# Weighting the first half's attention groups at the out-projection's operands, and its recurrent gates behind a later load

## The chip, the cores and the metric

One Trainium2 chip, one of its cores. The metric is the device time of one execution in microseconds (us). Engines are named as in the profile: PE (TensorE), DVE (VectorE), ACT (ScalarE), POOL (GpSimd), SP (SyncE, which here only issues DMAs). Each engine works through its own queue in order.

## What is computed

One layer over 2048 tokens of width 1024. The part that matters here is how the attention groups meet the output projection, and the gates of the recurrent mixer:

```python
def attention_mixer(q, k, v):                 # three groups g of two heads
    ...
    o = jnp.stack(outs, axis=2)
    lse = jnp.stack(lses, axis=2)
    alpha = jax.nn.softmax(lse, axis=2)       # shares of the groups
    return (o * alpha[..., None]).reshape(B, S, ATTN_WIDTH).astype(q.dtype)

def rg_lru(x, w_a, b_a, w_x, b_x, lam):
    r = jax.nn.sigmoid(jnp.einsum("bshi,hio->bsho", xh, w_a).reshape(B, S, C) + b_a)
    i = jax.nn.sigmoid(jnp.einsum("bshi,hio->bsho", xh, w_x).reshape(B, S, C) + b_x)
    ...                                       # a scan over the tokens
    mix = jnp.concatenate([y_attn, y_conv, y_lru], axis=-1)
    x = x + jnp.einsum("bsc,cd->bsd", mix, w_out)
    h2 = rmsnorm(x, norm2_g)
    ff = jnp.square(jax.nn.relu(jnp.einsum("bsd,df->bsf", h2, w_up)))
    return x + jnp.einsum("bsf,fd->bsd", ff, w_down)
```

## The kernel before

Activations lie with channels on the 128 partitions and tokens along the free axis. The tokens go in two halves h of 1024 (HS), each half in two blocks m of 512 (NB). Every float32 product is three matmuls of rounded halves: an operand is cast on ACT to its high half and DVE subtracts to get the low half (`split`, L242 and L243, in the input projection; `halves`, L907 and L908, behind it).

The order of the program: the input projection of half 0; then that of half 1, with the mixers of half 0 beside it; then output projection, up and down projections, with the mixers of half 1 as side work. The input projection's results are evacuated from PSUM by DVE (L388 to L395). In this stretch a planner lays out every engine's queue from priorities; the mixers of half 0 carry an offset that fills them in between the main matmuls. Within the mixers of half 0 the order is attention, convolution, recurrent mixer (`lru_mixer`), `combine`.

`combine` turns the statistics of the softmax, which it loads from `sscr` (L802), into the shares of the three groups and stores these to DRAM in `wscr` (L827). It then loads them back, broadcast over 64 partitions (L841), with each group's output from `oscr` (L843), multiplies on DVE (L834) and stores the product to `mscr` (L850, L854). `act_load` (L922) fetches `mscr` for the output projection into `rounded` slots, where `act_split` halves it.

`lru_mixer` takes three channel tiles t. It loads x from `lscr` (L542) and the gate weights from `gates_w` (L543), does a four-tap convolution on DVE (L548, L552), splits u block by block, runs two gates of three matmuls for each block on PE (L564 to L566), loads the GeLU branch from `gscr` (L571), and then does the scan (L582). `conv_ahead` loads the convolution input of half 1 from `uscr` (L464) and runs 31 taps on DVE (L472, L474) ahead of half 1's mixers. The values of half 1 are projected at L425 to L427, the last part of the input projection.

Small tiles come from a pool of 15 (`mtile`, `mtile_r`), large ones from a pool of 8 (`wide`). SP issues nearly all DMAs of half 0, POOL the key loads of the attention (L603, L612, L622) and the mixer loads of half 1; two copies of weights, `out_w` and `down_w`, are issued by ACT (L1590, L1591). A DMA signals one of eight semaphores of its kind (DMAHW0 to DMAHW7 for SP and ACT, DMASW0 to DMASW7 for POOL), taken in turn in the order in which the program issues them. An issue whose semaphore is still owed by an earlier DMA waits for that one.

Of the kernel before, what the change touches and what calls it, by code (L numbers as in the profile page):

```python
# [79 lines left out]
def body(tc, xt, w_in, w_v, w_out, w_up, w_down, vecs, lru_wa, lru_wx, consts, g_row, out, out_rows):  # L80
# [51 lines left out]
    def work(h):  # L132
        return wide_tile() if h == 0 else mtile()
# [4 lines left out]
    def work_pair(h):  # L138
        if h == 0:
            t = wp.tile([P, HS + 32], F32R, name="wr", tag="W")  # L140
            return t[:, :NB], t[:, NB:HS]
        return tuple(mp.tile([P, 544], F32R, name="mr", tag="M")[:, :NB] for _ in range(2))
# [310 lines left out]
    def loads(h):  # L453
        return nc.gpsimd if h else nc.sync
# [78 lines left out]
    def mtile_r():  # L533
        return mp.tile([P, 544], F32R, name="mr", tag="M")[:, :NB]

    def lru_mixer(h):
        n = HS if h == 0 else NB
        for t0 in range(h * HS, (h + 1) * HS, n):
            for t in range(3):
                x = work(h)  # L540
                gw = mtile_r()
                loads(h).dma_start(x[:, :n + 3], lscr[t][:, t0 + 29:t0 + n + 32])  # L542
                loads(h).dma_start(gw[:, :NB].bitcast(F32), gates_w[t])  # L543
                u = work(h)[:, :n]
                if h:
                    yield 0
                    yield 0
                nc.vector.tensor_scalar(u, x[:, 0:n], v("lru_conv_w", t * LTAPS), v("lru_conv_b", t), op0=OP.mult, op1=OP.add)  # L548
                for k in range(1, LTAPS):
                    if k == 2:  # L550
                        yield 1.3
                    nc.vector.scalar_tensor_tensor(u, x[:, k:k + n], v("lru_conv_w", t * LTAPS + k), u, op0=OP.mult, op1=OP.add)  # L552
                yield 1.5
                r, i = work(h)[:, :n], work(h)[:, :n]
                for c in range(0, n, NB):
                    uh, ul = work_pair(h)
                    split(u[:, c:c + NB], uh, ul)
                    yield 0.7
                    yield 0
                    for m, (dst, name) in enumerate(((r, "lru_ba"), (i, "lru_bx"))):  # L560
                        bank = mix_bank() if h and m else conv_bank()
                        wh, wl = (gw[:, part * P:(part + 1) * P] for part in (m, 2 + m))
                        with first():
                            nc.tensor.matmul(bank, wh, uh, start=True, stop=False)  # L564
                            nc.tensor.matmul(bank, wh, ul, start=False, stop=False)
                            nc.tensor.matmul(bank, wl, uh, start=False, stop=True)  # L566
                        nc.scalar.activation(dst[:, c:c + NB], bank, AF.Sigmoid, bias=v(name, t))
                    yield 0
                nc.vector.tensor_mul(u, u, i)
                gg = work(h)[:, :n]  # L570
                loads(h).dma_start(gg, gscr[t][:, t0:t0 + n])  # L571
                a = work(h)[:, :n]
                nc.scalar.activation(a, r, AF.Exp, scale=splus[:, 12 + t:13 + t])
                nc.scalar.activation(r, r, AF.Tanh, scale=splus[:, 9 + t:10 + t])
                yield 0.7
                nc.scalar.activation(i, a, AF.Square)
                nc.vector.scalar_tensor_tensor(r, i, 1.0, r, op0=OP.add, op1=OP.mult)
                nc.scalar.activation(r, r, AF.Sqrt)
                yield 0.7
                nc.vector.tensor_mul(u, u, r)  # L580
                init = 0.0 if t0 == 0 else state[:, t:t + 1]
                nc.vector.tensor_tensor_scan(i, a, u, init, OP.mult, OP.add)  # L582
                if t0 + n < S:
                    nc.vector.tensor_copy(state[:, t:t + 1], i[:, n - 1:n])
                yield 2.1
                nc.vector.tensor_mul(gg, gg, i)
                yield 0.7
                stores(h).dma_start(mscr[5 + t][:, t0:t0 + n], gg)
# [204 lines left out]
    def combine(h):  # L793
# [31 lines left out]
        for g in range(3):  # L825
            for j in range(2):
                stores(h).dma_start(wscr[g][j, t0:t0 + HS].rearrange("(c w) -> c w", w=16), m[j * HD:(j + 1) * HD, g, :])  # L827
        yield 0
        parts = [(b, g) for b in range(2) for g in range(3)]
        held = []  # L830

# [68 lines left out]
    def lo(i):  # L900
        return X(i)[:, NB:]

    def f32(a):
        return a.bitcast(F32)
# [10 lines left out]
    def out_at(n):  # L915
        return 1 - n // 4 % 2, n % 4 + n // 8 * 4

    def act_load(h, m, n0, n1):
        i, t0 = ACTS[m] + n0, h * HS + m * NB
        k = MIX_ORDER[n0]  # L920
        dst = rounded[i // 4].rearrange("p (s b n) -> p s b n", s=4, b=2)[:, i % 4:i % 4 + n1 - n0, 1, :]
        nc.sync.dma_start(f32(dst), mscr[k:k + n1 - n0, :, t0:t0 + NB].rearrange("k p n -> p k n"))  # L922

    def act_split(m, n):
        i = ACTS[m] + n
        halves(f32(lo(i)), hi(i), lo(i))

    def out_pair(w, pairs):
        if w in (2, 3):
# [790 lines left out]
```

## Time and profile before

| | |
|---|---|
| median of 3 runs | 2002.42 us (2000.58 to 2003.43) |
| the profiled execution, its time | 1999.48 us |
| its span, first to last instruction | 1997.7 us |
| granted TensorE clock, mean | 0.996 |
| instructions | 25490 |

The profiled execution is 2.9 us below the median, and 1.8 us of it lie around its span. Times in a timeline are from the start of the span. The stretch that the change touches lies between 255 and 510 us, the input projection of half 1, and between 490 and 530 us, the start of the output projection.

### The profile page before, as it was taken

The page shows a single profiled execution, that of the slowest core. Times are in us where ns is not written, and L with a number is a line of the kernel's source. Part 1 is how long each engine was busy: PE and PEld are TensorE (multiplying, and loading weights), DVE is VectorE, ACT ScalarE, POOL GpSimd, SP SyncE. Part 2 cuts the span into 40 slices and gives each one's busy share as a digit, 9 for nine tenths or more (in the row PEclk, how much of TensorE's full clock was granted, in tenths as well). Part 3 has the DMA queues.
Part 4 walks back from the last instruction along what each step waited for, and adds up shares of the span by engine and source line. Part 5 has one row for each costly group of instructions (what it writes and reads, how often), then busy time and mean ns, then how long its engine had stood idle before and what let it go on. Part 6 is the DMA issues. An engine that isn't in the chain of part 4 may idle for free.

```text
span 1997.7 us, 25490 instructions
## 1 busy us (share of the span) xinstructions
PE 1956.4 (98%) x8906; PEld 1593.7 (80%) x8906; DVE 1450.5 (73%) x1976; ACT 1050.4 (53%) x1634; POOL 168.2 (8%) x297
## 2 busy tenths in 40 slices
PE   8999998999999999999999999999999999999998
PEld 6887776789777777888888878788888888888886
DVE  7899785794567665887969899867555555577884
ACT  6144875513556764556656566446545555444343
POOL 0023200000022423000000000100000000000001
PEclk9999999999999999999999999999999999999999
DMA  5555596635555646544788777764444447786773
GB/s 169 165 151 159 165 294 196 216 121 165 182 168 164 196 151 217 193 154 162 271 286 279 249 275 248 245 199 146 158 153 151 145 143 262 240 293 215 263 260 136
DMA packets 202124, 399.78 MB, mean 200 GB/s; under 512 B 25382, under 2 KB 33814, under 8 KB 201932
## 3 DMA queue, kind: packets, MB, share of 16 engines
q1 hardware_dynamic: 182548, 342.02, 51.0%
q0 software_dynamic: 16096, 45.38, 7.8%
q10 hardware_dynamic: 3352, 10.76, 1.6%
q8 instruction: 70, 1.15, 0.2%
q14 instruction: 58, 0.48, 0.1%
HBM read 287.47 MB, written 119.00 MB: 203 GB/s over the span
## 4 chain that ended last, share of the span: by engine, by line
PE 82%; DVE 7%; DMA 5%; ACT 3%; issue 2%; SPq 0%; POOL 0%; DVEq 0%; ACTq 0%
PE bank L1135 10%; PE bank L1136 10%; PE bank L1137 10%; PE bank L1497 8%; PE bank L1498 8%; PE bank L1499 8%; PE mm L265 4%; PE mm L262 4%; PE mm L268 4%; PE bank L948 2%; PE bank L949 2%; PE bank L950 2%; DVE wide L474 1%; PE mm L425 1%; PE mm L427 1%
## 5 line engine op out<-in xcount | busy, mean ns | idle before, releaser
L1135 PE MATMUL bank<-rounded,pair 128*128 128x512 f32 x896 | 353.1, 394 | 2.8 <-ACT low L1144 2.2
L1136 PE MATMUL bank<-rounded,pair 128*128 128x512 f32 x896 | 351.7, 393 | 0.0
L1137 PE MATMUL bank<-rounded,pair 128*128 128x512 f32 x896 | 351.3, 392 | 0.0
L1497 PE MATMUL bank<-rounded,rounded 128*128 128x512 f32 x688 | 268.3, 390 | 1.7 <-DVE z L1510 1.4
L1499 PE MATMUL bank<-rounded,rounded 128*128 128x512 f32 x688 | 268.1, 390 | 0.0
L1498 PE MATMUL bank<-rounded,rounded 128*128 128x512 f32 x688 | 268.1, 390 | 0.0
L908 DVE TENSOR_TENSOR rounded<-rounded 128x1024 fp32r<-128x1024 f32 (+1 forms) x172 | 186.5, 1097 | 74.7 <-ACT rounded L907 73.6
L907 ACT CAST rounded<-rounded 128x1024 fp32r<-128x1024 f32 (+1 forms) x172 | 160.9, 949 | 134.5 <-DMA rounded<-fscr 102.8
L1135 PEld LDWEIGHTS bank<-rounded,pair 128*128 128x128 f32 x896 | 168.8, 188 | 41.5 <-ACT low L1144 2.6
L1137 PEld LDWEIGHTS bank<-rounded,pair 128*128 128x128 f32 x896 | 168.4, 188 | 35.9
L1136 PEld LDWEIGHTS bank<-rounded,pair 128*128 128x128 f32 x896 | 168.6, 188 | 34.9 <-issue 0.2
L262 PE MATMUL mm<-rounded,rounded 128*128 128x512 f32 x496 | 159.5, 397 | 8.4 <-ACT rounded L242 7.1
L268 PE MATMUL mm<-rounded,rounded 128*128 128x512 f32 x496 | 159.1, 396 | 0.0
L265 PE MATMUL mm<-rounded,rounded 128*128 128x512 f32 x496 | 157.4, 394 | 0.0
L907 ACT CAST rounded<-kept 128x1024 fp32r<-128x1024 f32 x80 | 84.1, 1051 | 133.7 <-DVE kept L1307 66.1
L1497 PEld LDWEIGHTS bank<-rounded,rounded 128*128 128x128 f32 x688 | 129.2, 188 | 29.3 <-DVE z L1510 1.8
L1499 PEld LDWEIGHTS bank<-rounded,rounded 128*128 128x128 f32 x688 | 129.2, 188 | 27.4 <-DVE rounded L908 0.4
L1498 PEld LDWEIGHTS bank<-rounded,rounded 128*128 128x128 f32 x688 | 129.2, 188 | 26.7
L242 ACT CAST rounded<-raw 128x512 fp32r<-128x512 f32 (+1 forms) x96 | 55.6, 582 | 146.8 <-PE mm L265 92.7
L907 ACT CAST pair<-wraw 128x1024 fp32r<-128x1024 f32 x64 | 67.1, 1048 | 117.1 <-PE bank L1136 111.2
L908 DVE TENSOR_TENSOR rounded<-kept,rounded 128x1024 fp32r<-128x1024 f32 x80 | 97.8, 1222 | 39.6 <-ACT rounded L907 39.3
L908 DVE TENSOR_TENSOR pair<-wraw,pair 128x1024 fp32r<-128x1024 f32 x64 | 78.2, 1222 | 60.6 <-ACT pair L907 60.5
(371 smaller groups left out, 3727.4 us busy)
## 6 DMA issues: line engine op xcount, KB each, us to landing
fscr<-low SPq DMA_DIRECT2D x224, 256.0 KB, 2.1
rounded<-fscr SPq DMA_DIRECT2D x112, 512.0 KB, 4.2
second<-in_w_down SPq DMA_DIRECT2D x80, 512.0 KB, 5.7
kept<-in_w_down SPq DMA_DIRECT2D x48, 512.0 KB, 5.4
raw<-in_w_in SPq DMA_DIRECT2D x64, 256.0 KB, 4.0
low<-in_w_up SPq DMA_DIRECT2D x64, 256.0 KB, 3.1
wraw<-in_w_up SPq DMA_DIRECT2D x64, 256.0 KB, 3.0
raw<-in_xt SPq DMA_DIRECT2D x32, 256.0 KB, 3.5
```

The source lines that it names most:

```text
L242: nc.scalar.copy(h, raw)
L262: nc.tensor.matmul(bank, wh[:, sl], ah[:, cols], start=first_, stop=False)
L265: nc.tensor.matmul(bank, wh[:, sl], al[:, cols], start=False, stop=False)
L268: nc.tensor.matmul(bank, wl[:, sl], ah[:, cols], start=False, stop=last_)
L907: nc.scalar.copy(h, raw)
L908: nc.vector.tensor_sub(l, raw, f32(h))
L1135: nc.tensor.matmul(bank, wh[:, sl], hi(x), start=fresh and k == 0, stop=False, **kw)
L1136: nc.tensor.matmul(bank, wh[:, sl], lo(x), start=False, stop=False, **kw)
L1137: nc.tensor.matmul(bank, wl[:, sl], hi(x), start=False, stop=k == KH - 1, **kw)
L1497: nc.tensor.matmul(banks[j], th[:, c], sh[:, x], start=fresh and k0, stop=False, **kw)
L1498: nc.tensor.matmul(banks[j], th[:, c], sl[:, x], start=False, stop=False, **kw)
L1499: nc.tensor.matmul(banks[j], tl[:, c], sh[:, x], start=False, stop=k1, **kw)
```

## The change

Two things change for half 0, and one of them also for half 1.

`combine(0)` ends with the stores of the shares to `wscr`. `act_load` puts the raw outputs of the groups from `oscr` straight into the operand slots (on SP) and loads the broadcast shares on POOL's queue into small tiles; `act_split` multiplies by the share (DVE) and halves the product. So the six L843 loads, the six `mscr` stores and two 768 KB loads go, six 256 KB loads on SP come; the twelve 128 KB broadcasts move from SP to POOL; the six multiplications stay, three of them now in the output projection's start.

`lru_mixer` splits both blocks of u first, then loads `gscr`, and then runs the gates; for half 0 the first matmul of each gate is planned behind that load by an order edge without a semaphore.

```diff
--- before.py
+++ after.py
@@ -533,6 +533,10 @@
     def mtile_r():
         return mp.tile([P, 544], F32R, name="mr", tag="M")[:, :NB]
 
+    def behind(i, other):
+        tc.add_manual_dep(i.ins, other.ins.name, mybir.DependencyInfo(
+            mybir.DependencyClass.NoSync, mybir.DependencyReason.DATA), reason="order")
+
     def lru_mixer(h):
         n = HS if h == 0 else NB
         for t0 in range(h * HS, (h + 1) * HS, n):
@@ -552,23 +556,28 @@
                     nc.vector.scalar_tensor_tensor(u, x[:, k:k + n], v("lru_conv_w", t * LTAPS + k), u, op0=OP.mult, op1=OP.add)
                 yield 1.5
                 r, i = work(h)[:, :n], work(h)[:, :n]
+                split_u = []
                 for c in range(0, n, NB):
-                    uh, ul = work_pair(h)
-                    split(u[:, c:c + NB], uh, ul)
+                    split_u.append(work_pair(h))
+                    split(u[:, c:c + NB], *split_u[-1])
                     yield 0.7
                     yield 0
+                gg = work(h)[:, :n]
+                loaded = loads(h).dma_start(gg, gscr[t][:, t0:t0 + n])
+                for c in range(0, n, NB):
+                    uh, ul = split_u[c // NB]
                     for m, (dst, name) in enumerate(((r, "lru_ba"), (i, "lru_bx"))):
                         bank = mix_bank() if h and m else conv_bank()
                         wh, wl = (gw[:, part * P:(part + 1) * P] for part in (m, 2 + m))
                         with first():
-                            nc.tensor.matmul(bank, wh, uh, start=True, stop=False)
+                            mm = nc.tensor.matmul(bank, wh, uh, start=True, stop=False)
+                            if h == 0:
+                                behind(mm, loaded)
                             nc.tensor.matmul(bank, wh, ul, start=False, stop=False)
                             nc.tensor.matmul(bank, wl, uh, start=False, stop=True)
                         nc.scalar.activation(dst[:, c:c + NB], bank, AF.Sigmoid, bias=v(name, t))
                     yield 0
                 nc.vector.tensor_mul(u, u, i)
-                gg = work(h)[:, :n]
-                loads(h).dma_start(gg, gscr[t][:, t0:t0 + n])
                 a = work(h)[:, :n]
                 nc.scalar.activation(a, r, AF.Exp, scale=splus[:, 12 + t:13 + t])
                 nc.scalar.activation(r, r, AF.Tanh, scale=splus[:, 9 + t:10 + t])
@@ -826,6 +835,8 @@
             for j in range(2):
                 stores(h).dma_start(wscr[g][j, t0:t0 + HS].rearrange("(c w) -> c w", w=16), m[j * HD:(j + 1) * HD, g, :])
         yield 0
+        if h == 0:
+            return
         parts = [(b, g) for b in range(2) for g in range(3)]
         held = []
 
@@ -915,15 +926,30 @@
     def out_at(n):
         return 1 - n // 4 % 2, n % 4 + n // 8 * 4
 
+    shares = {}
+
     def act_load(h, m, n0, n1):
         i, t0 = ACTS[m] + n0, h * HS + m * NB
         k = MIX_ORDER[n0]
+        if h == 0 and k < 3:
+            for n in range(n0, n1):
+                g = MIX_ORDER[n]
+                nc.sync.dma_start(f32(lo(ACTS[m] + n)), oscr[g][:, t0:t0 + NB])
+                w = shares[m, n] = mtile()[:, :NB]
+                for j in range(2):
+                    nc.gpsimd.dma_start(w[j * HD:(j + 1) * HD, :], wscr[g][j:j + 1, t0:t0 + NB].to_broadcast([HD, NB]))
+            return
         dst = rounded[i // 4].rearrange("p (s b n) -> p s b n", s=4, b=2)[:, i % 4:i % 4 + n1 - n0, 1, :]
         nc.sync.dma_start(f32(dst), mscr[k:k + n1 - n0, :, t0:t0 + NB].rearrange("k p n -> p k n"))
 
     def act_split(m, n):
         i = ACTS[m] + n
-        halves(f32(lo(i)), hi(i), lo(i))
+        x = f32(lo(i))
+        if (m, n) in shares:
+            w = shares.pop((m, n))
+            nc.vector.tensor_mul(w, w, x)
+            x = w
+        halves(x, hi(i), lo(i))
 
     def out_pair(w, pairs):
         if w in (2, 3):
```

On SP's queue, around the first load of gate weights, this stands before (names as in the text above; `raw` are input-projection weights):

```order
L922 DMA rounded_79<-mscr 128x2x512 [waits DMAHW5_49,DMAHW7_49,DMAHW3_49,PE_49]
L399 DMA uscr<-z 128x1024 [waits DMAHW4_49,DVE_49]
L251 DMA raw_102<-in_w_in 128x512 [waits DVE_49]
L251 DMA raw_103<-in_w_in 128x512 [waits DMAHW6_49,DVE_49]
L790 DMA sscr<-stat_142 512x1x4 [waits DVE_49,Activation_49]
L790 DMA sscr<-stat_142 512x1x4 [waits DMAHW0_49]
L543 DMA mr<-gates_w 128x512 [waits DMASW4_49,DMASW3_49,DMASW7_49,DMASW2_49,DMAHW1_49,DMASW1_49,DMASW0_49]
```

and this after the change (L943 is the old L922, L566 the old L571, L799 the old L790, L547 the old L543):

```order
L943 DMA rounded_79<-mscr 128x2x512 [waits DMAHW5_49,DMAHW7_49,DMAHW1_49,PE_49]
L566 DMA wide<-gscr 128x1024 [waits DMAHW6_49]
L399 DMA uscr<-z 128x1024 [waits DVE_49]
L251 DMA raw_102<-in_w_in 128x512 [waits DMAHW0_49,DVE_49]
L251 DMA raw_103<-in_w_in 128x512 [waits DVE_49]
L799 DMA sscr<-stat_142 512x1x4 [waits DMAHW2_49,DVE_49,Activation_49]
L799 DMA sscr<-stat_142 512x1x4 [waits DMAHW3_49]
L547 DMA mr<-gates_w 128x512 [waits DMASW4_49,DMASW3_49,DMASW7_49,DMASW2_49,DMAHW4_49,DMASW1_49,DMASW0_49]
```

The load of `gscr` has moved from behind the gates to ahead of the gate weights, and it, not the `uscr` store, now meets the semaphore (DMAHW6 here, DMAHW4 before) that ACT's `down_w` copy signals.

On DVE, from the third tile's last convolution tap (L552) to the split of its u for the first block's gates (the row with `wr`), this stood before; L580 and L582 are the second tile's scan and what leads to it (L582, the scan, is printed as SCALAR_TENSOR_TENSOR):

```order
L552 SCALAR_TENSOR_TENSOR wide<-wide,vec 128x1024 [waits DVE_49]
L834 TENSOR_TENSOR m<-m 128x512 [waits DMAHW6_49,DMAHW5_49,DMAHW1_49]
L834 TENSOR_TENSOR m<-m 128x512 [waits DMAHW4_49,DMAHW5_49,DMAHW3_49,DMASW1_49]
L580 TENSOR_TENSOR wide<-wide 128x1024 [waits Activation_49]
L388 SCALAR_TENSOR_TENSOR z<-mm,row_105 128x128x4 [waits PE_49] x2
L243 TENSOR_TENSOR rounded_83<-raw_102,rounded_83 128x512 [waits Activation_49]
L582 SCALAR_TENSOR_TENSOR wide<-wide 128x1024 [waits DVE_49]
L243 TENSOR_TENSOR wr<-wide,wr 128x512
```

and now, from the three products for token block 1 on (L950, which wait for POOL's loads; L556 is the old L552, L591 the old L582):

```order
L390 TENSOR_TENSOR z<-mm,row_105 128x512 [waits PE_49] x2
L243 TENSOR_TENSOR rounded_83<-raw_100,rounded_83 128x512 [waits Activation_49]
L950 TENSOR_TENSOR m<-m,rounded_80 128x512 [waits DMASW7_49,DMASW0_49]
L950 TENSOR_TENSOR m<-m,rounded_80 128x512 [waits DMASW2_49,DMASW1_49]
L950 TENSOR_TENSOR m<-m,rounded_80 128x512 [waits DMASW4_49,DMASW3_49]
L586 SCALAR_TENSOR_TENSOR wide<-wide 128x1024
L556 SCALAR_TENSOR_TENSOR wide<-wide,vec 128x1024 [waits DVE_49]
L243 TENSOR_TENSOR rounded_83<-raw_101,rounded_83 128x512 [waits DMAHW4_49,PE_49,Activation_49]
L589 TENSOR_TENSOR wide<-wide 128x1024 [waits Activation_49]
L243 TENSOR_TENSOR wr<-wide,wr 128x512 [waits DMAHW0_49,Activation_49]
L591 SCALAR_TENSOR_TENSOR wide<-wide 128x1024 [waits DVE_49]
L243 TENSOR_TENSOR wr<-wide,wr 128x512 [waits Activation_49]
```

The split of u has moved ahead of the second tile's scan. Three of the products stand ahead of it as two did before, but wait for loads on POOL's queue (DMASW) instead of SP's (DMAHW).

On SP, around the convolution's `uscr` load, before:

```order
L854 DMA mscr<-m 128x512 [waits DMAHW0_49,DVE_49]
L854 DMA mscr<-m 128x512 [waits DMAHW1_49,DVE_49]
L397 DMA zscr<-z 128x1024 [waits DMAHW2_49,DVE_49]
L251 DMA raw_102<-in_w_in 128x512 [waits DMAHW3_49,DVE_49]
L922 DMA rounded_80<-mscr 128x3x512 [waits DMAHW4_49,DMAHW6_49,DMAHW1_49,DMAHW0_49]
L588 DMA mscr<-wide 128x1024 [waits DMAHW5_49,DVE_49]
L251 DMA raw_103<-in_w_in 128x512 [waits DVE_49]
L571 DMA wide<-gscr 128x1024 [waits DMAHW7_49]
L922 DMA rounded_79<-mscr 128x2x512 [waits DMAHW5_49]
L464 DMA wide<-uscr 128x1054 [waits PE_49]
```

and now:

```order
L566 DMA wide<-gscr 128x1024 [waits DMAHW5_49,DVE_49]
L397 DMA zscr<-z 128x1024 [waits DMAHW6_49,DVE_49]
L597 DMA mscr<-wide 128x1024 [waits DMAHW7_49,DVE_49]
L251 DMA raw_102<-in_w_in 128x512 [waits DMAHW0_49,DVE_49]
L464 DMA wide<-uscr 128x1054 [waits DMAHW1_49]
L943 DMA rounded_79<-mscr 128x2x512 [waits DMAHW7_49,DMAHW2_49]
L251 DMA raw_103<-in_w_in 128x512 [waits DMAHW3_49,DVE_49]
```

The two L854 stores and the large `mscr` load of 128x3x512 are gone from ahead of L464.

## Rows read from the trace of the kernel before

**Rows 1.** The page of the profile, part 1, busy time by engine.

```profile
PE 1956.4 (98%) x8906; PEld 1593.7 (80%) x8906; DVE 1450.5 (73%) x1976; ACT 1050.4 (53%) x1634; POOL 168.2 (8%) x297
```

**Rows 2.** PE's waits, whole span: us in total, times, longest.

```profile
PE cb L564 <- DMA mr<-gates_w: 4.2, 1, 4.2
...
PE cb L565 <- DVE state L584: 1.9, 1, 1.9
PE mm L425 <- DVE z L393: 1.8, 1, 1.8
PE cb L564 <- ACT wr L242: 1.7, 2, 0.9
```

**Rows 3.** PE's timeline: start, us, line, idle time before and its releaser.

```profile
310.41 0.39 PE L265 MATMUL mm<-rounded,rounded 128*128 128x512 f32 x1
314.98 0.76 PE L564 MATMUL cb<-wr,mr 128*128 128x512 f32 x1 [4.18 <-DMA mr<-gates_w]
...
367.77 0.50 PE L564 MATMUL cb<-wr,mr 128*128 128x512 f32 x1 [0.89 <-ACT wr L242]
...
374.70 0.50 PE L565 MATMUL cb<-wr,mr 128*128 128x512 f32 x1 [1.87 <-DVE state L584]
...
443.25 0.44 PE L425 MATMUL mm<-rounded,rounded 128*128 128x384 f32 x1 [1.79 <-DVE z L393]
```

**Rows 4.** SP's queue, timeline: start and duration of each issue.

```profile
304.88 0.33 SPq L399 DMA_DIRECT2D uscr<-z  x1
...
308.09 0.44 SPq L543 DMA_DIRECT2D mr<-gates_w  x1
...
380.27 0.47 SPq L464 DMA_DIRECT2D wide<-uscr  x1
```

**Rows 5.** Waits of SP's queue between 250 and 400 us.

```profile
SPq L251 <- DVE rounded L243: 16.0, 12, 3.4
...
SPq L399 <- DMA down_w<-in_w_down: 9.3, 1, 9.3
```

**Rows 6.** Line L543, the gate weights: us from issue to landing.

```profile
DMA to landing us min/median/max: 5.7/7.2/8.5
```

**Rows 7.** Stretches: us, busy time by engine, granted clock, DMA share.

```profile
305.00:307.00 2.00, 2.00 (x11) 1.31 (x9) 0.38 (x3) 0.95 (x5) 0.00 (x0) 1.00 0.68 244
...
330.00:370.00 40.00, 38.26 (x166) 30.25 (x165) 32.24 (x39) 24.19 (x28) 3.89 (x7) 1.00 0.89 273
...
445.00:448.00 3.00, 3.00 (x11) 3.00 (x10) 1.12 (x2) 0.74 (x2) 0.00 (x0) 0.50 0.99 350
448.00:450.00 2.00, 2.00 (x12) 2.00 (x12) 0.00 (x0) 0.47 (x1) 0.00 (x0) 0.96 0.58 185
```

**Rows 8.** DVE's timeline.

```profile
344.41 1.22 DVE L586 TENSOR_TENSOR wide<-wide 128x1024 f32<-128x1024 f32 x1
...
352.80 0.69 DVE L834 TENSOR_TENSOR m<-m 128x512 f32<-128x512 f32 x1 [0.48 <-DMA m<-oscr]
...
387.04 0.80 DVE L472 TENSOR_SCALAR wide<-wide,vec 128x1024 f32<-128x1024 f32 x1
...
442.51 1.28 DVE L393 TENSOR_TENSOR z<-mm,row 128x512 f32<-128x512 f32 x2
```

**Rows 9.** Line L827 on SP, stores of the shares: ns of an issue, landing.

```profile
L827 SPq DMA_DIRECT2D wscr<-m x6: 446/591/596, 327.7 to 331.2; - x6
...
DMA to landing us min/median/max: 2.6/2.8/3.1
```

**Rows 10.** Line L841 issued on POOL's queue, second half.

```profile
L841 POOL DMA_DIRECT2D m<-wscr x12: 522/532/546, 763.5 to 780.6; - x12
...
DMA to landing us min/median/max: 2.7/6.3/7.8
```

**Rows 11.** POOL's timeline.

```profile
362.19 1.06 POOL L612 DMA_DIRECT2D mr<-zscr  x2 [12.07 <-PE mm L268]
...
530.19 1.21 POOL L603 DMA_DIRECT2D m<-zscr  x2 [63.36 <-PE cb L721]
```

## The prediction

> **What bounds the kernel now.** The page comes first: PE is busy for 98% of the span [rows 1]. So the change can only give what PE waits for, or what its clock loses, in the stretch that it touches. The waits of PE over the whole span name what there is [rows 2]: 4.2 us for the first tile's gate weights, 1.7 us in two waits for the cast of u, 1.9 us at a gate's second matmul, and 1.8 us at the value projection, together 9.6 us. PE's timeline places them [rows 3]: at 314.98, at the second tile (1.7 less the 0.89 at 367.77, so 0.85), at 367.77 and 374.70 (both third tile) and at 443.25. A gap also costs clock behind it: after the last one 11 matmuls took 3.00 us at a granted clock of 0.50 (the 1.2 GHz level), where the next 12 took 2.00 us near full clock (2.4 GHz) [rows 7]. That is 11 x (0.273 - 0.167) = 1.2 us; behind 314.98 I take the same, and it stays as long as that gap does.
>
> Elsewhere I give the change nothing. What it removes (20 issues of SP net, 3 MB of transfers) is no work of PE, and the counts of matmuls, DVE and ACT operations do not change. The moved products cost DVE 0.69 us each [rows 8].
>
> **The first gates (A).** The weights that end the 4.18 us are late because SP stands 9.3 us on the semaphore of the `down_w` copy [rows 5] and goes on at 304.88; the weights' issue follows 3.21 us later, at 308.09, and they land 6.89 us behind that, where PE starts [rows 3, 4]. After the change SP still meets that copy, now with the `gscr` load, and this load stands ahead of the weights. It adds one issue, priced as the weights' own 0.44 us [rows 4], and 512 KB in front of them, 1.7 us at 307 GB/s (273 GB/s at a DMA share of 0.89, between 330 and 370 [rows 7]). The gates start 2.1 us later. The order puts them two main matmuls later, at 0.23 us each (38.26 us / 166 [rows 7]), work that PE does ahead of the wait instead of behind it. So PE's whole program moves by 2.1 - 0.45 = +1.7 us. The lower bound is 0: between 305 and 307 the DMA share was only 0.68 [rows 7], so the 512 KB may fit beside the rest. The upper bound is +5.0: the two `oscr` loads now issued ahead of the copy can hold it back by their 512 KB, another 1.7 us, and the weights can take the 8.5 us that the slowest of the three took [rows 6], 1.6 more. The planned edge to the `gscr` load itself costs nothing, since the weights behind it are what arrives last.
>
> **The second tile (B).** Both splits of u now precede its gates, in the program and on DVE and ACT; PE comes to them some matmuls earlier as well. Which of the two gains more no row tells, so I take half of the 0.85 us, -0.4, with 0 and -0.85 as bounds.
>
> **The third tile (C).** Its two waits are 0.89 + 1.87 = 2.76 us. The second, named after L584, is the split of u that stands behind the previous tile's scan in DVE's queue; the order shows it ahead of the scan now. What comes in front instead is three products that wait for POOL's broadcasts. When these land I follow from the shares, without the shift A, which moves all of it. In the order the shares are computed behind L586, which ended at 345.63 [rows 8]: with a subtraction of 0.69 us and five small operations, say 347. Six stores at 0.59 us an issue end at 350.6 and land 2.8 us later, 353.4 [rows 9]; the last broadcast takes 0.53 us to issue and lands 6.3 us later (the same broadcast on POOL's queue in half 1 [rows 10]), at 360.2. Three products end at 362.3; then come five operations to the low half of u, two of 0.69 and three of some 1.23 us as L586, to 367.4. PE came to these gates at 366.88 (367.77 - 0.89 [rows 3]); they stand four matmuls earlier (-0.9), B takes 0.4, and the matmul that wants the low half is two further (+0.45): 366.0. The wait is 1.4 us in place of 2.76: -1.4. With the fastest landing of 2.7 us there is no wait (-2.8); with the slowest of 7.8 us it is 2.9 (+0.1) [rows 10].
>
> **The convolution and the value projection (D).** At 442.51 DVE evacuates late, behind the 31 taps that began at 387.04, when the `uscr` load, issued at 380.27, had landed [rows 4, 8]. In the order that load no longer stands behind two `mscr` stores and the 768 KB load that waits for them. It goes out several us earlier, ahead of the taps' place in DVE's queue; 1.8 us earlier are enough to end the gap at 443.25. That gives 1.79 + 1.2 of clock = -3.0 us; the other bound is 0.
>
> **What is hidden.** The last three products, for block 0, fall into the start of the output projection, three times 0.69 us on DVE where PE still works on the value projection; uncovered they would cost 2.1. POOL's broadcasts for block 0 stand in front of half 1's keys until the operand slots are free, near the start of the output projection; POOL idles 63 us before its next set at 530.19 [rows 11], so I count nothing there.
>
> **Sum.** +1.7 - 0.4 - 1.4 - 3.0 = -3.1 us. On the profiled execution, whose time is 1.8 us more than its span, 1999.48 becomes 1996.4. The median of the runs lies 2.9 us above that execution, so I forecast 2002.42 - 3.1 = 1999.3 us. About 0.2%, 4.0 us, is what a measurement of this kernel can tell from no change.
>
> **A rule that speaks against it.** POOL's issues took 1.06 us for two at 362.19 [rows 11], in a stretch where DVE was busy 32.24 of 40 us [rows 7], as much each as the 0.53 us of the broadcasts in half 1 [rows 10]. So DVE does not slow POOL's issue here by these rows.
>
> The Trainium skill (SBUF — State Buffer, section "SBUF: two separate sides") says that GpSimd cannot write the descriptors of its own DMAs while DVE runs an operation in a mode that takes both ports, and that a DMA from SP's or ACT's queue is free of this. The two rows above show no such hold; by the rule the products would come late.
>
> **Rivals.**
> - *POOL held by DVE.* If POOL could work only while DVE idles, a share of 1 - 32.24/40 = 0.19, six issues of 0.53 us would take 16.5 us instead of 3.2. The broadcasts would come 13 us later, PE would stand at the third tile's gates for that, and the clock would fall there too: -3.1 + 13 + 1.2 = +11, 2013.5. From about 6 us of delay the result is slower by the bound above. The issue at 362.19 speaks against it. Chance 0.05.
> - *Late shares (slower).* The last two stores of the shares stand on SP behind an L251 load that waits for DVE, as 12 of them did, up to 3.4 us [rows 5]. If that is its wait, if all six broadcasts then go out only behind the last store (2.1 us more) and land in 7.8 instead of 6.3 us [rows 10], they come 7.0 us later: -3.1 + 7.0 + 1.2 = +5.1, 2007.5. The point is again some 6 us. For it: three DMA queues hang on each other, where all was on SP before. Against: the twelve waits come to 16.0 us, 1.3 us each. Chance 0.14.
> - *The first gates eat it.* A at its upper bound gives +0.2, 2002.6. Chance 0.12.
> - *The value projection still waits.* If DVE's queue stays full to 445 whatever the start of the taps, D is 0: -0.1, 2002.3. Chance 0.11.
> - *All waits go but the first.* A at 0, B, C and D at their best give -6.6, 1995.8. For it: 3 MB less beside a DMA share of 0.89 between 330 and 370 [rows 7]. Chance 0.20.
>
> **How the numbers follow.** The likeliest case, the sum, has 0.38; its own range is 1996.5 to 2001.5, and two fifths of it (0.15) lie below the bound of 1998.4. Faster: 0.15 + 0.20 = 0.35. Within 0.2%: 0.23 + 0.12 + 0.11 = 0.46. Slower: 0.14 + 0.05 = 0.19. The range from 1995 to 2007.5 takes in every case but POOL held by DVE and the upper half of the late shares, with a little left below.
>
> **What would show it.** In the profile after: the wait for `gates_w` at 5 to 7 us and the first gate near 317 (A); a wait for the cast at the second tile of about 0.4 (B); at the third tile one wait of 1 to 2 us at the gate's second matmul, with DVE waiting for `m<-wscr` ahead of the products (C); the taps starting by 381 and no wait at the value projection, its clock staying at the upper level (D). The prediction is wrong if PE waits over 5 us at the third tile, if the wait at the value projection stays, or if new waits appear behind 490 us.

## The result and the profile after

The changed kernel takes 2005.23 us (median of 20 runs, 2000.89 to 2011.25), the kernel before 2000.96 us beside it (20 runs): a ratio of 1.0023 [1.0014, 1.0031]. It is slower, by some 4.6 us by the ratio (the medians are 4.3 us apart), where 3.1 us less was forecast. The time lies inside the range, on the side that had the smallest chance. The ratios below leave out one execution, of 3943.42 us, of the kernel with the copy in eight pieces.

The profile taken with it fell on one of its long runs (span 2008.4 us, time 2010.17). A second one, of the first experiment, has a span of 2004.9 us and a time of 2006.74; it is nearest to the median, and the steps below are read from it unless the text says otherwise. Against the profile of before (span 1997.7 us) it is 7.2 us longer; the out-projection's first matmul starts at 512.63 instead of 509.11 us, so 3.5 of them lie ahead of it, in the stretch that the change touches. The executions profiled differ by more than the medians do: this one lies 1.5 us above its median, the one of before 1.5 us below.

First the waits of PE in the first profile after, whole span (us in total, times, longest):

```profile
PE cb L573 <- DMA mr<-gates_w: 11.1, 1, 11.1
...
PE cb L573 <- ACT wr L242: 1.7, 1, 1.7
PE bank L974 <- DVE z L393: 1.4, 1, 1.4
PE cb L573 <- ACT wide L578: 1.3, 2, 0.8
PE mm L425 <- DVE z L393: 1.3, 1, 1.3
```

Every place named by [rows 2] still has a wait. The first has grown from 4.2 to 11.1 us, the value projection's is 1.3 in place of 1.8, and L974, the first matmul of the out-projection, is new. PE's timeline of the second profile gives the places:

```profile
318.98 0.80 PE L573 MATMUL cb<-wr,mr 128*128 128x512 f32 x1 [8.05 <-DMA mr<-gates_w]
...
348.14 0.50 PE L573 MATMUL cb<-wr,mr 128*128 128x512 f32 x1 [0.55 <-ACT wide L578]
...
371.01 0.50 PE L573 MATMUL cb<-wr,mr 128*128 128x512 f32 x1 [1.55 <-ACT wr L242]
...
372.70 0.50 PE L576 MATMUL cb<-wr,mr 128*128 128x512 f32 x1 [0.96 <-DVE wr L243]
...
376.96 0.50 PE L573 MATMUL cb<-wr,mr 128*128 128x512 f32 x1 [0.76 <-ACT wide L578]
...
446.30 0.44 PE L425 MATMUL mm<-rounded,rounded 128*128 128x384 f32 x1 [1.52 <-DVE z L393]
...
512.63 0.47 PE L974 MATMUL bank<-rounded,pair 128*128 128x512 f32 x1 [1.02 <-DVE z L393]
```

Against [rows 3]: the first gate 4.0 us later; the second tile's wait down from 0.85 to 0.55; the third tile in three waits of 3.27 us together where there were 2.76; the value projection still waiting. SP's queue in the same profile shows what the first gates wait for, and how the shares' stores and the `uscr` load go out:

```profile
305.70 0.33 SPq L566 DMA_DIRECT2D wide<-gscr  x1
...
310.30 0.42 SPq L547 DMA_DIRECT2D mr<-gates_w  x1
...
350.85 2.38 SPq L836 DMA_DIRECT2D wscr<-m  x4
355.45 0.34 SPq L251 DMA_DIRECT2D raw<-in_w_in  x1
355.83 1.08 SPq L836 DMA_DIRECT2D wscr<-m  x2
...
361.67 9.60 SPq L251 DMA_DIRECT2D raw<-in_w_in  x2
...
379.42 0.85 SPq L464 DMA_DIRECT2D wide<-uscr  x1
```

Behind the gap at 446.30 the clock no longer falls, as the stretch that follows shows (columns as in [rows 7]):

```profile
446.00:449.00 3.00, 2.70 (x15) 2.58 (x16) 0.84 (x2) 0.00 (x0) 0.00 (x0) 1.00 1.01 344
```

DVE's timeline has the three products (L950), the split behind them (L243) and the first tap (L472):

```profile
354.73 0.69 DVE L243 TENSOR_TENSOR rounded<-raw,rounded 128x512 fp32r<-128x512 f32 x1 [4.05 <-ACT rounded L242]
...
361.72 0.69 DVE L950 TENSOR_TENSOR m<-m,rounded 128x512 f32<-128x512 f32 x1
362.63 0.69 DVE L950 TENSOR_TENSOR m<-m,rounded 128x512 f32<-128x512 f32 x1 [0.21 <-DMA m<-wscr]
367.28 0.69 DVE L950 TENSOR_TENSOR m<-m,rounded 128x512 f32<-128x512 f32 x1 [3.96 <-DMA m<-wscr]
...
370.22 0.68 DVE L243 TENSOR_TENSOR rounded<-raw,rounded 128x512 fp32r<-128x512 f32 x1
...
385.54 0.81 DVE L472 TENSOR_SCALAR wide<-wide,vec 128x1024 f32<-128x1024 f32 x1 [6.53 <-DMA wide<-uscr]
```

And POOL's, with the six broadcasts of the shares:

```profile
355.68 2.13 POOL L940 DMA_DIRECT2D m<-wscr  x4 [90.42 <-DVE rounded L243]
359.73 0.52 POOL L940 DMA_DIRECT2D m<-wscr  x1 [1.92 <-PE mm L268]
362.70 0.52 POOL L940 DMA_DIRECT2D m<-wscr  x1 [2.45 <-DMA wscr<-m]
```

Read together: the last two stores of the shares stand on SP behind an L251 load of weights, which goes out only when DVE's split at 354.73 has freed a buffer, and that split had waited 4.05 us for ACT. The last broadcast goes out at 362.70, and the third product stands 3.96 us for it at the head of DVE's queue. Everything behind it in that queue is late, the split at 370.22 above all. SP stands in the two L251 loads from 361.67 to 371.27. Between them and the `uscr` load stand a `zscr` store, an `mscr` store and a third L251 load, which SP issues at 377.34, 378.43 and 379.04, each as DVE ends what it waits for. So the `uscr` load goes out at 379.42, only 0.85 us earlier than before [rows 4]. DVE then waits 6.53 us for it ahead of the taps.

### The profile page after: what moved, and what is told of

Its sections match the earlier page's. It is cut to its first block, busy times and chain, and to the rows that moved or that the text cites. A ratio compares the mean times of both kernels' runs of the same rounds, so it can differ in the third digit from the quotient of the medians.

```text
span 2008.4 us, 25466 instructions
## 1 busy us (share of the span) xinstructions
PE 1957.6 (97%) x8906; PEld 1592.1 (79%) x8906; DVE 1450.2 (72%) x1976; ACT 1051.3 (52%) x1634; POOL 174.5 (9%) x309
## 4 chain that ended last, share of the span: by engine, by line
PE 74%; DMA 9%; DVE 7%; ACT 6%; issue 3%; SPq 0%; POOL 0%; DVEq 0%; ACTq 0%; POOLq 0%
PE bank L1161 9%; PE bank L1162 9%; PE bank L1163 9%; PE bank L1525 7%; PE bank L1523 7%; PE bank L1524 7%; PE mm L268 4%; PE mm L265 4%; PE mm L262 4%; DMA raw<-in_xt 2%; PE bank L975 2%; PE bank L976 2%; PE bank L974 2%; DVE rounded L919 1%; ACT rounded L918 1%
```

## The experiments

Each was timed in five rounds; ratios are to the kernel before, beside it on the same chip, with a 95% interval. An expectation gives what each theory then open makes of the run. The two main ones: the first gates carry the loss, since their weights come late on SP; or the shares carry it, since the products hold DVE's queue.

**The changed kernel again**, for a second profile and interval.

> The changed kernel once more, as the common measure of the others. Theory 1 (the first gates): the weights' wait on PE is again the largest of its stretch, 8 to 11 us, and the kernel 0.1 to 0.4% slower than before. Theory 2 (the shares on POOL's queue): the first wait varies, but the loss sits at the third tile and behind 490 us.

2006.91 us, ratio 1.0028 [1.0017, 1.0039]. Its profile is the one read above.

**The recurrent mixer's part alone**: the kernel before with the new `lru_mixer` and `behind`, the shares as they were.

> Only the recurrent mixer's part on the kernel before. Theory 1: the gscr load stands ahead of the gate weights but the down_w copy lands near 305 as before, so PE's wait for the weights is 6 to 8 us in place of 4.2, and the time 2 to 4 us above before; the wait at the value projection stays. Theory 2: the time equals before within 1 us, since no share is loaded on POOL's queue.

2002.08 us, 1.0007 [0.9999, 1.0016]. The wait for the gates' weights is 8.22 us, so its growth belongs to this part. There is no wait at the third tile at all: planned this way the gates lose the 2.76 us of before when no product that waits stands in front of the split (one stands there, at 364.91, and does not wait). But the taps start at 385.00, the `uscr` load still ends a wait of DVE's there (2.21 us), and the value projection waits 4.02 us, 2.2 more than before. Gains and losses nearly cancel.

**The shares' part alone**: the kernel before with `shares`, the products and the early loads, the old `lru_mixer`.

> Only the shares' part, the recurrent mixer as before. Theory 1: SP goes on some 3 us later than before because the oscr loads stand ahead of the copy, the wait for the weights is 6 to 8 us, and with what the removed traffic gives back the time lies within 2 us of before. Theory 2: the time is 4 us or more above before, as after the whole change.

2007.68 us, 1.0034 [1.0021, 1.0047]: this part alone is at least as slow as the whole change. The first gates wait 4.13 us, as before. What costs here are the second and third tile, in PE's timeline:

```profile
345.34 0.50 PE L564 MATMUL cb<-wr,mr 128*128 128x512 f32 x1 [2.04 <-ACT wr L242]
...
373.94 0.80 PE L564 MATMUL cb<-wr,mr 128*128 128x512 f32 x1 [4.57 <-ACT wr L242]
```

and in DVE's, where the convolution of each tile waits for its `lscr` load and the products for the broadcasts:

```profile
330.83 0.81 DVE L548 TENSOR_SCALAR wide<-wide,vec 128x1024 f32<-128x1024 f32 x1 [4.66 <-DMA wide<-lscr]
...
357.77 0.69 DVE L941 TENSOR_TENSOR m<-m,rounded 128x512 f32<-128x512 f32 x1 [3.46 <-DMA m<-wscr]
360.69 0.69 DVE L941 TENSOR_TENSOR m<-m,rounded 128x512 f32<-128x512 f32 x1 [2.22 <-DMA m<-wscr]
365.13 0.81 DVE L548 TENSOR_SCALAR wide<-wide,vec 128x1024 f32<-128x1024 f32 x1 [1.96 <-DMA wide<-lscr]
```

The second tile's `lscr` load is not late: it goes out at 325.48 us, and in the kernel before at 328.84. But its first tap (L548) now stands ahead of four evacuations and other work on DVE that it followed before, and waits for the load at the head of the queue. In the changed kernel these waits are not there. So the two parts are no sum: the mixer's part repairs some of what the shares' part breaks.

**The copy in eight pieces**, meant to let SP go on earlier:

```
-nc.scalar.dma_start(down_w, w_down[0:2 * KT, :, 0:NB])
+for kp in range(KT):
+    nc.scalar.dma_start(down_w[2 * kp:2 * kp + 2], w_down[2 * kp:2 * kp + 2, :, 0:NB])
```

> The changed kernel with ACT's one copy of 4 MB to down_w cut into eight of 512 KB, so that no semaphore of SP's is owed by a copy of 40 us. Theory 1: SP does not stand 9 us ahead of the gscr load, the gate weights land before PE comes to them or within 2 us of it, and the time is 6 to 10 us below that of the changed kernel, below before. Theory 2: the wait goes, but less than half of the loss comes back.

2017.48 us, 1.0078 [1.0062, 1.0095]. The wait at the first gates falls to 2.90 us, but the pieces wait for each other on ACT, and ACT computes nothing meanwhile. ACT's timeline and PE's, one row each:

```profile
293.11 1.28 ACT L361 ACT_TABLE_LOAD   x1 [24.01 <-DMA down_w<-in_w_down]
```

```profile
295.15 1.37 PE L262 MATMUL mm<-rounded,rounded 128*128 128x512 f32 x2 [17.71 <-ACT row L361]
```

So this run says nothing on the first gates' price. The copy had to move elsewhere.

**The products late**: of the changed kernel, each product is ordered behind the last DVE instruction that stands in the program where the out-projection starts.

```
         w = shares.pop((m, n))
-        nc.vector.tensor_mul(w, w, x)
+        behind(nc.vector.tensor_mul(w, w, x), last_dve[0])
...
+    last_dve[0] = next(i for i in reversed(nc.cur_bb.bb.instructions) if i.engine == mybir.EngineType.DVE)
     with tc.issue_after(last_act):
```

> The changed kernel with one more planner edge: the products of block 1 stand behind the last evacuation of the input projection's columns that the program has issued by then, instead of ahead of the third tile's split. Theory S (DVE's queue, held by the last share's broadcast): the third tile's waits fall from 3.3 us to under 1, the wait at the value projection from 1.5 to under 0.5, and the time is 3 to 5 us below the changed kernel's, about that of before plus 1. Rival (the first gates alone make the loss): the time stays within 1 us of the changed kernel's.

1998.58 us, 0.9984 [0.9973, 0.9996]: faster than the kernel before, and 0.44% below the changed kernel's second run (0.28 to 0.60% by the two intervals), more than was expected. Nothing else was edited, though the planner's order on SP moves with it: the third tile's `gscr` load goes out at 365.20, between the two L251 loads, instead of at 372.07. The wait at the first gates is as in the changed kernel (8.02 us), the third tile has none, and the value projection has none. Its DVE and SP timelines show why; first DVE:

```profile
365.66 0.69 DVE L243 TENSOR_TENSOR rounded<-raw,rounded 128x512 fp32r<-128x512 f32 x1 [0.49 <-ACT rounded L242]
...
381.74 0.81 DVE L472 TENSOR_SCALAR wide<-wide,vec 128x1024 f32<-128x1024 f32 x1
```

then SP:

```profile
361.71 0.34 SPq L251 DMA_DIRECT2D raw<-in_w_in  x1
...
366.38 0.33 SPq L251 DMA_DIRECT2D raw<-in_w_in  x1
...
375.21 0.45 SPq L464 DMA_DIRECT2D wide<-uscr  x1
```

The split comes at 365.66 instead of 370.22, SP's second L251 load at 366.38, the `uscr` load 4.2 us earlier than in the changed kernel; DVE does not wait for it, and the taps begin 3.8 us earlier. The products in DVE's queue are what turned the sign.

**The copy late**, in the changed kernel and in the one before: it leaves ACT's queue and goes out on POOL's at about 364 us, behind the PE instruction that is the last at that point.

```
-        nc.scalar.dma_start(down_w, w_down[0:2 * KT, :, 0:NB])
...
+        if n == 10:
+            last_pe = next(i for i in reversed(nc.cur_bb.bb.instructions) if i.engine == mybir.EngineType.PE)
+            copy = nc.gpsimd.dma_start(down_w, w_down[0:2 * KT, :, 0:NB])
+            tc.add_manual_dep(copy.ins, last_pe.name, mybir.DependencyInfo(
+                mybir.DependencyClass.NoSync, mybir.DependencyReason.DATA), reason="order")
```

> The changed kernel with the 4 MB copy to down_w issued by POOL behind its last key loads near 366 us, ahead of a wait of 97 us, instead of by ACT at 268. Theory G (the first gates are late because SP meets the copy's semaphore): the wait for the gate weights falls from 8 us to under 1, and the time is 6 to 9 us below the changed kernel's, 1 to 4 below before. Rival (contention): the copy slows the loads around it wherever it runs, and less than 3 us come back.

> The kernel before with the same move of the copy. Theory G: its wait of 4.2 us for the gate weights goes, with the clock behind it, and the time is 4 to 6 us below before. Rival: within 1 us of before, since SP meets another late transfer or the copy slows the convolution's load.

2010.59 us, 1.0044 [1.0028, 1.0059] in the changed kernel, and 2010.97 us, 1.0050 [1.0034, 1.0065] in the one before. SP's stand on the copy is gone, but the wait at the first gates is still 3.01 and 3.45 us. What it gave is lost behind it: the first run's rival holds, and of the second's expectations neither does. DVE's row and PE's, of the changed kernel with the late copy:

```profile
388.73 0.81 DVE L472 TENSOR_SCALAR wide<-wide,vec 128x1024 f32<-128x1024 f32 x1 [13.59 <-DMA wide<-uscr]
```

```profile
449.34 0.69 PE L425 MATMUL mm<-rounded,rounded 128*128 128x384 f32 x1 [5.12 <-DVE z L393]
```

In the kernel before with it the taps start at 397.20 and the value projection waits 6.78 us. The copy now runs beside the `mscr` stores and the `uscr` load. In the changed kernel that load goes out 3.0 us earlier than without the move, at 376.38, but DVE gets it 12.3 us later instead of 6.1; in the kernel before SP stands on loads of `mscr` ahead of it, and it goes out only at 391.02. So the copy costs the kernel before 0.5% more here than at its old place; in the changed kernel the difference, 0.16%, is within the intervals.

**Products and copy late, and the `gscr` load behind the gates.** All three edits at once (the third is the one shown next).

> Products late as in the run with one more planner edge, the gscr load back behind the gates, and the copy late. Theories S and G together: no wait above 1 us on PE between 300 and 500 us, time 8 to 10 us below before. If only G holds, 3 to 5 us below before; if neither, at before or above.

2010.65 us, 1.0047 [1.0030, 1.0063]. The shortest wait at the first gates of all (2.65 us) and, as in the run with the copy late in the changed kernel, a `uscr` load that lands late: it goes out at 379.33, DVE waits 14.11 us for it, the value projection 6.45 us. A wait of PE that is taken away at 315 us is worth nothing while the value projection hangs on that load.

**Products late, the `gscr` load behind the gates.** To the products' edit comes:

```
-                gg = work(h)[:, :n]
-                loaded = loads(h).dma_start(gg, gscr[t][:, t0:t0 + n])
...
-                            if h == 0:
-                                behind(mm, loaded)
...
                 nc.vector.tensor_mul(u, u, i)
+                gg = work(h)[:, :n]
+                loads(h).dma_start(gg, gscr[t][:, t0:t0 + n])
```

> All products late, and the gscr load back behind the gates. Theory A (the load ahead of the weights makes 4 of the 8 us of their wait): the wait for the gate weights falls from 8.0 to 4 to 5 us, and the time is 3 to 4 us below the run with the products late alone. Rival: the wait stays near 8, since the down_w copy's landing sets it, and the time is within 1 us.

1999.96 us, 0.9989 [0.9975, 1.0003]. The wait at the first gates is 6.27 instead of 8.02 us. The weights reach PE 6.61 us behind their issue instead of 8.31: the 512 KB ahead of them cost the 1.7 us that the prediction gave them. The time gains nothing by it. The taps start at 383.43 (381.74 with the products late alone), and 1.27 us of wait come back at the value projection.

**Block 0's products behind the last evacuation as well**: the same `last_dve` line at the start of `out_second`.

> As the run with the gscr load behind, and the products of block 0 behind the last evacuations of the input projection. The wait of the output projection's first matmul, 1.0 to 1.6 us for an evacuation, goes, and the time is 1 to 2 us lower; rival: a product for block 0 comes late and PE waits there.

1999.17 us, 0.9984 [0.9970, 0.9999]. The wait at the out-projection's first matmul is 0.88 us (1.09 without the line), and the time is the same within the interval. DVE's timeline shows the products behind the evacuation (L393) now, and still a late evacuation:

```profile
504.24 1.23 DVE L917 TENSOR_TENSOR rounded<-rounded 128x1024 fp32r<-128x1024 f32 x1 [5.02 <-ACT rounded L916]
505.39 2.48 DVE L393 TENSOR_TENSOR z<-mm,row 128x512 f32<-128x512 f32 x4
507.78 1.89 DVE L949 TENSOR_TENSOR m<-m,rounded 128x512 f32<-128x512 f32 x3
```

It stands behind a subtraction of a split that waits 5.02 us for ACT. So the wait comes without the products as well; here that subtraction stands ahead of the evacuation.

**Products late with the old `lru_mixer`.**

> The shares' part with all products late, and the recurrent mixer as before. If splitting both blocks first helps (theory B and C): second and third tile wait 2 to 3 us together as before, and the time is 2 to 4 us above the run with the gscr load behind. If it does not: within 1 us of it.

2007.97 us, 1.0031 [1.0016, 1.0046], as the shares' part alone. The second and third tile wait 2.83 and 3.15 us, and DVE waits 5.45 and 3.75 us for the `lscr` loads. So late products gain nothing with the old mixer. That these two waits are the reason is not shown: with the new mixer and the `gscr` load behind the gates the third tile's is there too, 3.33 us, and the time holds.

**The third product of each block alone late**, since it alone waited 3.96 us:

```
+            mul = nc.vector.tensor_mul(w, w, x)
+            if not [q for q in shares if q[0] == m]:
+                behind(mul, last_dve[0])
```

> The changed kernel with only the third product of block 1 planned late; the first two stay ahead of the third tile's split. Theory S (the wait for the last broadcast, 4.0 us, holds DVE's queue): nearly the whole gain of moving all three, the time 6 to 9 us below the changed kernel's and 0 to 3 below before. Rival (the products' own 2 us on DVE): a third of the gain.

2002.64 us, 1.0000 [0.9986, 1.0014]: 0.28% of the 0.44% that late products give, with intervals too wide to tell it from the whole gain or from a third. In the profile, of the longest run, DVE now waits 2.05 us at the first two products, the third tile 1.06 us, the value projection 0.97 us. So the rows show a wait left where the slow broadcast is out of the way; that the place of all three costs, and not one slow broadcast, the times do not show.

## Why the prediction was wrong

By its own steps, in the changed kernel's second profile:

| step | forecast | measured | how |
|---|---|---|---|
| A, first gates | +1.7 | +3.55 | 318.98 - 314.98, less the 0.45 for the two matmuls |
| B, second tile | -0.4 | -0.3 | 0.55 for 0.85 |
| C, third tile | -1.4 | +0.5 | 1.55 + 0.96 + 0.76 for 2.76 |
| D, value projection | -3.0 | -1.5 | gap 1.52 for 1.79; the clock stays up behind it, 1.2 as forecast |
| out-projection's start, "hidden" | 0 | +1.0 | the new wait at L974 |
| sum | -3.1 | +3.25 | out-projection starts 3.5 later |

**C is the step that turned the sign**, with part of D hanging on it. The chain was named rightly (three products ahead of the split, waiting for POOL's broadcasts), but the last broadcast was put at 360.2 us before the shift A, 363.8 with the shift as measured, and the product that waits for it started at 367.28. Two terms of its sum were too small. The six stores were priced as one stretch of issues; the last two waited behind an L251 load, at 355.83 where the fourth ended at 353.23, and the sixth ended at 356.91, 2.8 us later than the sum with the shift has it. This is the mechanism of the rival of the late shares, to which I gave 0.14. And the landing of the last store was put at 2.8 us, from its issue's end, where POOL went on 5.8 us behind it, at 362.70. The trace puts POOL's last 2.45 us of waiting down to that store, and its single packets bear that out: of the 384 packets of 64 bytes that are the six stores, the first 256 had ended at 354.56, the last of the other 128 at 361.32, 5.0 us behind the sixth store's issue at 356.32. With the products late the last ended at 361.18 and POOL issued at 362.43; with the third alone late, at 364.73 and 365.90. Why the last packets are so late is not settled. The broadcast itself landed sooner than priced, 4.5 us from its start for 6.8. That product waited 3.96 us at the head of DVE's queue. The late products, the one edit that undoes this, are worth 0.44%.

POOL was not held by DVE: it issued four broadcasts in 2.13 us from 355.68, each 0.53 us, as in half 1 [rows 10], while DVE was busy for 1.97 of the 2 us from 355.

The Trainium skill (SBUF — State Buffer, section "SBUF: two separate sides") says that GpSimd cannot write descriptors while DVE runs an operation in a mode that takes both ports. The products came late as that rule would have it, but these issues show no such hold, and the last broadcast waited for a store.

**D** took it as given that the `uscr` load goes out several us earlier because fewer transfers stand ahead of it on SP. SP is an in-order queue, and what stood ahead were loads and stores that wait for DVE, 9.60 us in two L251 loads from 361.67 and more up to 379.37; the work they wait for stands behind the products. The load was 0.85 us earlier, below the 1.8 us that the prediction itself asked for.

Those 1.8 us were misread as well. Before, the load did not hold the taps: DVE came to the first one (387.04 [rows 8]) straight from a split, behind two evacuations that had waited for PE.

```profile
384.57 2.03 DVE L390 TENSOR_TENSOR z<-mm,row 128x512 f32<-128x512 f32 x2 [4.20 <-PE mm L268]
386.43 0.69 DVE L243 TENSOR_TENSOR rounded<-raw,rounded 128x512 fp32r<-128x512 f32 x1
```

Now the taps start 1.5 us earlier, but two such evacuations, a split and one tap more stand between their start and the evacuation that ends the wait: DVE works for 60.2 us there instead of 55.8. So an earlier start by 1.8 us was not enough. Where the products are late, the load goes out 5.1 us earlier than in the kernel before, the taps start 5.3 us earlier, and the gap is gone. With the `gscr` load behind the gates they start 3.6 us earlier, with block 0's products late too 5.5, and gaps of 1.27 and 1.25 us are left: DVE's stretch is 59.1 us there, and in the second PE comes to it 2.1 us sooner than before. In the changed kernel the clock stays up behind the gap, as forecast, though the gap that the prediction took for the cause of its fall is still there (1.52 us): that 1.2 us came right by luck.

From the taps' start to the value projection's resumption it is 56 to 61 us in every kernel that waits there: 56.2 before, 60.8 after, 60.7 with the mixer's part alone, for starts from 381.5 to 397.2. That is why an earlier first gate alone buys nothing (the `gscr` load behind the gates): unless the taps start earlier, what is saved at 315 us is waited for at 443.

**A** had the right mechanism and, for the 512 KB of the `gscr` load, the right price: 1.7 us (8.31 - 6.61, from the weights' issue to PE's start, with the products late). In the changed kernel the weights took 8.68 us for 6.89 before, +1.8. Mis-sized were the other two terms. The copy landed in 38.0 us instead of 37.1 (+0.8 at SP, put at nothing). And the weights were issued 4.60 us behind SP's release instead of 3.21, +1.4 where 0.44 stood: 0.37 for the `gscr` load's issue, and the two loads and two `sscr` stores between took 1.71 and 1.64 instead of 1.25 each pair. In the first profile after, the copy took 40.2 us, and the gates started at 322.37. With the same 0.45 taken off, A is +6.9 there, beyond the upper bound of +5.0.

**B** was right. **The hidden work** was not hidden: the out-projection's first matmul waits 1.02 us for an evacuation. That step counted what the products take on DVE; it did not ask where the evacuation stands among them and the splits. By the prediction's own marks (the wait at the value projection stays, a new wait behind 490 us) it is wrong.

**Open.** The other 3.7 us of the 7.2 in this profile lie behind the out-projection's start, in code that the change touches only at its beginning, by block 0's products, and in half 1's recurrent mixer, where the `gscr` load goes out earlier. By the medians, 4.3 us apart, some 3 us of the 7.2 belong to the two executions that were profiled. PE's listed waits behind 520 us come to 13.1 us here and 9.9 before, spread over the banks of the feed-forward and out-projection. From the out-projection's first matmul to the end it is 1488.6 us before and 1486.9 to 1494.0 in the other profiles (1492.3 and 1491.5 in the two of the changed kernel, 1489.6 with the products late, 1493.7 with the third product late). The four kernels with the old `lru_mixer` have 1486.9 to 1490.4 us, the ten profiles with the new one 1489.6 to 1494.0. Half 1's load is not the whole of it: in three of the ten it is back in its old place, and they have 1490.6 to 1494.0. No experiment was made on it.

## What to carry to other kernels

An operation that is moved into an in-order queue ahead of what others wait for costs not its 0.69 us but the latest of its operands: ask of every moved instruction what its slowest input is, and what stands behind it on its engine and, through buffers, on the queues. An early issue in a program is no early issue on a queue whose head waits for a buffer; follow each load back to what frees the slot of the transfer ahead of it. A row that starts without a wait was held by its place in the queue, and an earlier operand gains nothing there. And before a gap is counted as a gain, look for the wait further on that will take it back (here the taps' start, 60 us ahead of the value projection).

## What the runs showed of the hardware

The 4 MB copy from DRAM to DRAM landed in 37.1 to 40.2 us on ACT's queue at 267 to 270 us, where loads for PE ran beside it, and in 23.3 to 24.2 us from POOL's queue at 363 to 366 us, where its issue took 1.06 us. In eight pieces it stopped ACT's computing for 24 us: issues that wait for a semaphore held back what stands behind them on that engine. A store of 4 KB in 64 packets of 64 bytes, issued at 356.32 us, had its last packet end 5.0 us later in the changed kernel's second profile, and 7.0 us later with the third product late (from 357.72 to 364.73).
